# Filter taps of the next quarter computed between a convolution's forward and inverse transform, and a parameter tile that is 24 bytes longer

## The chip, the core and the metric

The kernel runs on one core of a Trainium2 chip. The metric is the device time of one execution in microseconds (us). The core's engines run side by side and meet at semaphores: TensorE (PE in the profile, with its weight loads listed as PEld), VectorE (DVE), ScalarE (ACT), GpSimd (POOL) and SyncE (SP, here only an issuer of transfers). Matrix products go from the on-chip memory SBUF through PE into PSUM, eight banks of 512 floats for each partition. DVE and ACT read PSUM and write SBUF.

## The reference

One encoder layer over 512 tokens of width 2048 in float32. The input is normalised, projected, and goes through two branches: a Hyena branch with long filters and grouped attention. The branches are gated and merged, projected again, and a feed-forward part follows. The part that the change touches is the long convolution over 1024 channels and the filter that it needs:

```python
def implicit_filter(L, w1, b1, w2, b2, w3, b3, w4, freq):
    ...
    h = jnp.sin(fr * (h @ w3.astype(f32) + b3.astype(f32)))
    h = h @ w4.astype(f32)
    ...
    decay = jnp.exp(-t[:, None] * deltas[None, :])
    h_fwd = h[:, :HYENA_W] * decay
    h_bwd = h[:, HYENA_W:] * decay
    k = jnp.concatenate([h_fwd, jnp.zeros((1, HYENA_W), f32), h_bwd[:0:-1]], axis=0)
    return k / jnp.sum(jnp.abs(k), axis=0, keepdims=True)

def bidir_fft_conv(u, k):
    L = u.shape[1]
    uf = jnp.fft.rfft(u.astype(jnp.float32), n=2 * L, axis=1)
    kf = jnp.fft.rfft(k, n=2 * L, axis=0)
    return jnp.fft.irfft(uf * kf[None], n=2 * L, axis=1)[:, :L]

def hybrid_layer(x, ...):
    h = rms_norm(x, mix_norm_g)
    proj = h @ w_in
    ...
    x0, x1, hv = jnp.split(u_h, HYENA_ORDER + 1, axis=-1)
    z = hv * x1
    z = (bidir_fft_conv(z, filt) + hy_bias * z)
    y_h = z * x0
    ...                                   # attention y_a, gates g_h, g_a
    merged = g_h * (y_h @ w_br_hyena) + g_a * (y_a @ w_br_attn)
    x = x + merged @ w_out
    h2 = rms_norm(x, ffn_norm_g)
    return x + (jax.nn.silu(h2 @ w_ffn_gate) * (h2 @ w_ffn_up)) @ w_ffn_down
```

## The kernel before

**Products.** Activations stand in SBUF with channels on the 128 partitions and the 512 tokens along them. Every float32 operand is split into a high part of fewer bits and the rest, each of type fp32r: ACT writes the high part (`wh`, `..h`, line 176 for weights, line 197 for activations), DVE the rest (`wl`, `..l`, lines 177 and 198). A product is then three matmuls, high by high, high by low and low by high (`mm3`). All matmuls are issued by `mm`, line 125, and all transposes on PE at line 128, in the order in which the program is written. Weights come in raw tiles `wr` of eight 128x128 blocks, in the order of use. Such a tile feeds 24 matmuls. A row `x2` in the listings below is two matmuls in a row with the same names.

**Stages.** The main stream on PE has these stages, one behind another, by the names of their results: `px` and `phv` (the Hyena projections, in four quarters of 256 channels), `kv` and `q` (attention, with `av`), `b` (branches), `g` (gates), `o` (output projection), `f` (feed-forward gate and up), `d` and `e` (down). In `g`, `f` and the two parts of the down projection, 2x2 blocks of a product are computed by seven products in place of eight (the function `seven`). These have eight X operands `X0` to `X7` that stay in SBUF (`fX0` and so on); for each block of weights there are eight matmuls 512 wide, one for each X, and eight 256 wide for the low part. Their names in the trace are `gx`, `gy`, `gz`, `fx` and so on.

**The side queue.** What the long convolutions need is written as generators. They stand in one queue, and `step()` is called once after each product (three matmuls) of the main stream. It runs the generator at the head to its next `yield n`, and then lets n steps pass. So a `yield 6` is 18 matmuls of the main stream between two parts of side work. Nothing else sets the order on PE.

For each quarter q two generators stand in the queue. `filter_gen(q)` computes the taps: `fp` is the last layer of the filter network (`hh`, `hl` its hidden values, `w4s` its weights), multiplied by the decay into `fd` and `bd` (line 356); ACT sums their absolute values, DVE makes the factor `rn` and the half sums `hs` and `hd` (lines 371 and 372). Then it pauses, transposes the half sums (`ktp`), transforms them (`kp`, with cosines and sines `CS`) and stores the spectrum `K` in device memory `kd`. `conv_gen(q)` transposes the signal, transforms it (`up`), multiplies it by the spectrum on DVE into `Y` (lines 449 to 454), and splits that into `Yt<q><fb><ph>h` and `..l`. After a `yield 6` the inverse transform runs in two halves of 16 matmuls each, `ab<q><ph><c>`, which read these splits; ACT and DVE scale and add the result into `abs` (lines 475 and 477).

**Where tiles lie.** SBUF pools are stacks from the left and from the right of each partition's memory, and each tile takes its bytes rounded up to 32. The first tile on the left is `prm` (parameters by channel, 175 floats a partition). Above it come the small constants, the weight tiles (`wr`, `wh`, `wl`), the temporary tiles, the activations of each stage, and later the split weights of the seven-product stages, all on the left. On the right lie, from the `g` stage on, a small `pad` tile, the raw tiles `wq`, and X operands in `xa` and `vp`; later `ea` with a part of the activations for `d`.

Of the kernel before, what the change touches and what calls it, by code (L numbers as in the profile page):

```python
# [11 lines left out]
F32 = mybir.dt.float32  # L12
# [5 lines left out]
P = 128  # L18
S = 512
# [4 lines left out]
NQ = 4  # L24
# [34 lines left out]
NPC = _n  # L59
# [47 lines left out]
def layer_kernel(tc, wpk, xT, par, flt, zemb, w4, decT, tb2, rope, qkg, out):  # L107
# [3 lines left out]
    cpool = tc.alloc_tile_pool(name="cpool", bufs=1)  # L111
# [9 lines left out]
    def ps_tile(name):  # L121
        return banks["pool"].tile([P, S], F32, tag="ps", bufs=banks["n"], name=name)

    def mm(out, lhsT, rhs, start, stop, **kw):
        tc.keep_in_program_order(nc.tensor.matmul(out, lhsT=lhsT, rhs=rhs, start=start, stop=stop, **kw))  # L125

    def transpose(out, src):
        tc.keep_in_program_order(nc.tensor.transpose(out, src, ident))
# [25 lines left out]
    def queue(gen):  # L154
        side["queue"].append(gen)

    def tmp(name):
        return tpool.tile([P, S], F32, tag="tmp", bufs=5, name=name)

# [34 lines left out]
    def split(pool, src, th, tl, bh, bl, name):  # L194
        hi = pool.tile([P, S], F32R, tag=th, bufs=bh, name=name + "h")
        lo = pool.tile([P, S], F32R, tag=tl, bufs=bl, name=name + "l")
        nc.scalar.copy(hi, src)
        nc.vector.tensor_tensor(lo, src, hi.bitcast(F32), ALU.subtract)
        return hi, lo
# [18 lines left out]
        return y  # L218


    prm = cpool.tile([P, NPC], F32, name="prm")
    nc.scalar.dma_start(prm, par)
    warm = cpool.tile([P, 1], F32, name="warm")
    nc.vector.memset(warm, 0.0)
# [2 lines left out]
    def pcol(name, i=0):  # L227
        a = PC[name] + i
        return prm[:, a:a + 1]
# [40 lines left out]
    def cw(name, shape, tag, bufs=1, dt=F32):  # L270
        return cv.tile(shape, dt, tag=tag, bufs=bufs, name=name)

    def work(name):
        return cw(name, [P, S], "wk", 6)

    fl = cw("fl", [P, 324], "fl")[:, :260]
    nc.scalar.dma_start(fl, flt)
    zem = tmp("zemb")
    nc.scalar.dma_start(zem[:33], zemb)
# [2 lines left out]
    def part(i, low, a, b):  # L282
        return CS[i][:, low * S + a:low * S + b]
# [37 lines left out]
            if l == 0:  # L321
                w4_parts(0)

    filt, kd = {}, {}
    w4t = {}

    def w4_load(q):
        w4t[q] = tmp(f"w4r{q}")
        for h in range(2):
            nc.scalar.dma_start(w4t[q][h * 64:(h + 1) * 64], w4[q])  # L330

    def w4_parts(q):

        w4r = w4t[q]
        w4h = tpool.tile([P, S], F32R, tag="tmp", bufs=5, name=f"w4h{q}")
        w4s = cw(f"w4s{q}", [P, 512], "w4s", 1, F32R)
        nc.scalar.copy(w4h[64:], w4r[64:])
        nc.scalar.copy(w4s[:64], w4r[:64])
        nc.vector.tensor_tensor(w4s[64:], w4r[64:], w4h[64:].bitcast(F32), ALU.subtract)
        w4t[q] = w4s  # L340

    def filter_gen(q):

        w4s = w4t.pop(q)
        rn, hs_l, hd_l = [], [], []
        for c in range(2):
            dec = cw(f"dec{q}{c}", [P, S], "dec", 1)
            nc.scalar.dma_start(dec, decT[2 * q + c])
            fd = work(f"fd{q}{c}")
            bd = cw(f"bd{q}{c}", [P, S + 1], "bd", 1)  # L350
            for half, dst in ((0, fd), (1, bd[:, :S])):
                fp = ps_tile(f"fp{q}{c}{half}")
                csl = slice(half * 256 + c * P, half * 256 + (c + 1) * P)
                mm(fp, w4s[:, csl], mlp["h"][0], True, False)
                mm(fp, w4s[:, csl], mlp["h"][1], False, True)
                nc.vector.tensor_tensor(dst, fp, dec, ALU.mult)
                yield 2
            nc.vector.memset(bd[:, S:S + 1], 0.0)
            n2 = cw(f"n2{q}{c}", [P, 2], "n2", 2)
            scr = tmp(f"scr{q}{c}")  # L360
            nc.scalar.activation(scr, fd, AF.Abs, accum_out=n2[:, 0:1])
            nc.scalar.activation(scr, bd[:, 1:], AF.Abs, accum_out=n2[:, 1:2])
            r = cw(f"rn{q}{c}", [P, 1], "rn", 4)
            nc.vector.tensor_tensor(r, n2[:, 0:1], n2[:, 1:2], ALU.add)
            nc.vector.tensor_scalar(r, r, 256.0, None, ALU.mult)
            nc.vector.reciprocal(r, r)
            rn.append(r)

            hs, hd = work(f"hs{q}{c}"), work(f"hd{q}{c}")
            for h, op in ((hs, ALU.add), (hd, ALU.subtract)):  # L370
                nc.vector.tensor_tensor(h[:, :256], fd[:, ::2], bd[:, 2::2], op)
                nc.vector.tensor_tensor(h[:, 256:], fd[:, 1::2], bd[:, 1:S:2], op)
            hs_l.append(hs)
            hd_l.append(hd)
        if q + 1 < NQ:
            w4_load(q + 1)
        yield 8 if q else 12
        if q + 1 < NQ:
            w4_parts(q + 1)
        taps = []  # L380
        for i, src in enumerate((hs_l, hd_l)):
            for j in range(2):
                tp = ps_tile(f"ktp{q}{i}{j}")
                for n in range(4):
                    o = n // 2 * 256 + j * P
                    transpose(tp[:, n * P:(n + 1) * P], src[n % 2][:, o:o + P])
                taps.append(split(cv, tp, "kh", "kl", 4, 4, f"k{i}{q}{j}"))
            yield 3
        yield 6


        kd[q] = dpool.tile([256, 6 * 256], F32, tag=f"kd{q}", bufs=1, name=f"kd{q}")
        for fb in range(2):
            g = []
            for i in range(2):
                kp = ps_tile(f"kp{q}{fb}{i}")
                for j in range(2):
                    a = j * 256 + fb * P
                    mm3(kp, part(i, 0, a, a + P), part(i, 1, a, a + P), *taps[2 * i + j], j == 0, j == 1)
                g.append(kp)  # L400
                yield 2
            cr, ci = tmp(f"kcr{q}{fb}"), tmp(f"kci{q}{fb}")
            nc.scalar.activation(cr, g[0], AF.Copy, scale=pcol("cosw", fb))
            nc.scalar.activation(ci, g[1], AF.Copy, scale=pcol("cosw", fb))
            k1, k2, k3 = (work(f"K{i}{q}{fb}") for i in range(3))
            nc.vector.scalar_tensor_tensor(k1, g[1], pcol("sinw", fb), cr, ALU.mult, ALU.add)
            nc.vector.scalar_tensor_tensor(k2, g[0], pcol("nsinw", fb), ci, ALU.mult, ALU.add)
            nc.vector.scalar_tensor_tensor(k3[:, :256], g[1][:, 256:], pcol("nsinw", fb), cr[:, 256:], ALU.mult, ALU.add)
            nc.vector.scalar_tensor_tensor(k3[:, 256:], g[0][:, 256:], pcol("sinw", fb), ci[:, 256:], ALU.mult, ALU.add)
            rows = kd[q][fb * P:(fb + 1) * P]  # L410
            nc.gpsimd.dma_start(rows[:, :S], k3)
            for i, k in enumerate((k1, k2)):
                nc.gpsimd.dma_start(rows[:, S:].rearrange("p (a b c) -> p a b c", a=2, b=2)[:, :, i],
                                    k.rearrange("p (a c) -> p a c", a=2))
        filt[q] = rn
# [3 lines left out]
    def conv_gen(q):  # L419

        rn = filt[q]
# [12 lines left out]
        for fb in range(2):  # L434
# [10 lines left out]
            for ph in range(2):  # L445
# [8 lines left out]
                nc.vector.tensor_tensor(y.rearrange("p (f c) -> p f c", f=2), u[:, 0], u[:, 1], ALU.add)  # L454
                ys[ph, fb] = split(r3, y, "r", "r", 16, 16, f"Yt{q}{fb}{ph}")
                yield 5
        yield 6
        abs_ = [work(f"abs{2 * q + c}") for c in range(2)]
        for ph in range(2):
            ab = [ps_tile(f"ab{q}{ph}{c}") for c in range(2)]  # L460
            for fb in range(2):
                yhi, ylo = ys[ph, fb]
                for c in range(2):
                    for i in range(2):
                        csl = slice(i * 256 + c * P, i * 256 + (c + 1) * P)
                        a = fb * 256
                        both = CS[i].rearrange("p (h t) -> p h t", h=2)[:, :, a:a + P]
                        o = ab[c][:, i * 256:(i + 1) * 256]
                        mm(o, yhi[:, csl], both, fb == 0 and i == 0, False, skip_group_check=True)
                        mm(o[:, :P], ylo[:, csl], part(i, 0, a, a + P), False, fb == 1 and i == 1, skip_group_check=True)  # L470
            yield 2
            for c in range(2):
                low = tmp(f"abl{q}{ph}{c}")[:, :256].rearrange("p (i t) -> p i t", i=2)
                src = ab[c].rearrange("p (i h t) -> p i h t", i=2, h=2)
                nc.scalar.activation(low, src[:, :, 1], AF.Copy, scale=rn[c])
                dst = abs_[c].rearrange("p (i s t) -> p i s t", i=2, s=2)[:, :, ph]
                nc.vector.scalar_tensor_tensor(dst, src[:, :, 0], rn[c], low, ALU.mult, ALU.add)
# [15 lines left out]
    xps = [ps_tile(f"px{i}") for i in range(XW)]  # L493
    xg, acc1 = [], work("acc1")
    queue(mlp_gen())
    queue(filter_gen(0))
    w00 = wblk()
    for k in range(KT):
# [887 lines left out]
```

## Time and profile before

| | us |
|---|---|
| median of 3 runs | 2547.15 |
| lowest and highest | 2546.93, 2549.27 |
| profiled execution | 2545.9 |
| its span, first to last instruction | 2544.1 |
| mean granted clock of PE | 0.998 of full |

The profile is of one execution. A row of waits names the engine, what it was about to run, the instruction that let it go, and the us in total, the number of times and the longest. A row of a window has the stretch (us from the start of the span), its length, then for each of PE, PEld, DVE, ACT and POOL the busy us and the number of instructions, then PEclk (1.00 is full speed), the busy share of the transfer engines, and GB/s. A row of a timeline has start, us, engine, line, operation, result and operands. A matmul of 512 columns shows 0.39 us from start to end, but consecutive ones overlap: the spacing of their starts is what they cost.

### The profile page before, as it was taken

The page shows a single profiled execution, that of the slowest core. Times are in us where ns is not written, and L with a number is a line of the kernel's source. Part 1 is how long each engine was busy: PE and PEld are TensorE (multiplying, and loading weights), DVE is VectorE, ACT ScalarE, POOL GpSimd, SP SyncE. Part 2 cuts the span into 40 slices and gives each one's busy share as a digit, 9 for nine tenths or more (in the row PEclk, how much of TensorE's full clock was granted, in tenths as well). Part 3 has the DMA queues.
Part 4 walks back from the last instruction along what each step waited for, and adds up shares of the span by engine and source line. Part 5 has one row for each costly group of instructions (what it writes and reads, how often), then busy time and mean ns, then how long its engine had stood idle before and what let it go on. Part 6 is the DMA issues. An engine that isn't in the chain of part 4 may idle for free.

```text
span 2544.1 us, 34631 instructions
## 1 busy us (share of the span) xinstructions
PE 2522.7 (99%) x13246; PEld 2151.3 (85%) x13246; DVE 2071.8 (81%) x2933; ACT 1180.5 (46%) x1755; POOL 176.6 (7%) x287
## 2 busy tenths in 40 slices
PE   9999999999999999999999999999999999999999
PEld 7878788888888888888888888888888888888888
DVE  7788884856569999654899899989998988987887
ACT  5433333655445454443544444444444445445443
POOL 0000001110000000000000000000000002001111
PEclk9999999999999999999999999999999999999999
DMA  6334343222544434644333333333333349647754
GB/s 211 119 107 135 123 138 114 81 89 98 185 151 159 152 137 158 203 157 149 112 104 125 116 123 126 110 131 116 125 125 116 119 148 218 165 125 188 181 153 116
DMA packets 113282, 350.42 MB, mean 138 GB/s; under 512 B 13723, under 2 KB 15003, under 8 KB 112892
## 3 DMA queue, kind: packets, MB, share of 16 engines
q1 hardware_dynamic: 70128, 248.02, 29.7%
q0 software_dynamic: 22576, 63.19, 9.3%
q10 hardware_dynamic: 20412, 37.00, 4.7%
q8 instruction: 104, 1.70, 0.3%
q14 instruction: 62, 0.51, 0.1%
HBM read 297.56 MB, written 54.26 MB: 138 GB/s over the span
## 4 chain that ended last, share of the span: by engine, by line
PE 92%; DVE 5%; issue 1%; ACT 1%; POOL 0%; DVEq 0%; ACTq 0%; POOLq 0%
PE fx L125 19%; PE fy L125 10%; PE o L125 7%; PE px L125 7%; PE b L125 6%; PE gx L125 6%; PE d L125 5%; PE fz L125 5%; PE dx L125 3%; PE ex L125 3%; PE q L125 3%; PE gy L125 3%; PE phv L125 2%; PE ey L125 2%; PE dy L125 2%; PE gz L125 2%
## 5 line engine op out<-in xcount | busy, mean ns | idle before, releaser
L177 DVE TENSOR_TENSOR wl<-wr,wh 128x1024 fp32r<-128x1024 f32 (+1 forms) x168 | 201.0, 1198 | 137.9 <-ACT wh L176 137.1
L176 ACT CAST wh<-wr 128x1024 fp32r<-128x1024 f32 (+1 forms) x168 | 173.3, 1032 | 297.2 <-PE o L125 66.4
L861 ACT CAST fwhs<-fs 128x1024 fp32r<-128x1024 f32 x176 | 184.7, 1049 | 93.5 <-PE fz L125 69.9
L863 DVE TENSOR_TENSOR fwls<-fs,fwhs 128x1024 fp32r<-128x1024 f32 x176 | 214.7, 1220 | 15.2 <-ACT fwhs L861 15.1
L861 ACT CAST fwha<-fa 128x1024 fp32r<-128x1024 f32 x132 | 138.8, 1052 | 153.9 <-PE fx L125 84.6
L125 PE MATMUL px<-xh,wh 128*128 128x512 f32 x576 | 183.3, 400 | 0.0
L125 PE MATMUL fx<-fX,fwhs 128*128 128x512 f32 x704 | 178.0, 395 | 0.6 <-DVE fv L893 0.6
L125 PE MATMUL fy<-fX,fwhs 128*128 128x512 f32 x704 | 178.2, 395 | 0.0
L125 PE MATMUL fx<-fX,fwha 128*128 128x512 f32 x704 | 174.7, 395 | 1.3 <-DVE c L990 1.3
L863 DVE TENSOR_TENSOR fwla<-fa,fwha 128x1024 fp32r<-128x1024 f32 x132 | 161.4, 1223 | 10.2 <-ACT fwha L861 9.6
L125 PE MATMUL o<-ms,wh 128*128 128x512 f32 x512 | 157.8, 389 | 0.0
L125 PEld LDWEIGHTS fx<-fX,fwha 128*128 128x128 f32 x704 | 129.1, 188 | 29.0 <-issue 1.9
L125 PEld LDWEIGHTS fx<-fX,fwhs 128*128 128x128 f32 x704 | 129.1, 188 | 28.1 <-DVE fv L893 0.9
L125 PEld LDWEIGHTS fy<-fX,fwhs 128*128 128x128 f32 x704 | 129.0, 188 | 27.4 <-DVE fv L893 0.4
L125 PEld LDWEIGHTS px<-xh,wh 128*128 128x128 f32 x576 | 108.9, 192 | 24.5 <-issue 2.4
L125 PE MATMUL d<-act,wh 128*128 128x512 f32 x384 | 120.5, 395 | 0.0
L125 PE MATMUL px<-xh,wl 128*128 128x512 f32 x288 | 114.2, 397 | 0.0
L125 PEld LDWEIGHTS o<-ms,wh 128*128 128x128 f32 x512 | 96.1, 188 | 20.0
L854 DVE TENSOR_TENSOR fs<-fa,fa 128x1024 f32<-128x1024 f32 x88 | 107.4, 1220 | 4.6 <-DMA fa<-wpk 2.4
L854 DVE TENSOR_TENSOR fs<-fs,fa 128x1024 f32<-128x1024 f32 x88 | 107.3, 1220 | 0.9 <-PE o L125 0.2
L125 PE MATMUL o<-ms,wl 128*128 128x512 f32 x256 | 99.7, 389 | 0.0
L125 PE MATMUL fx<-fX,fwls 128*128 128x256 f32 x704 | 97.4, 281 | 0.2 <-DVE fwls L863 0.2
(1088 smaller groups left out, 5917.7 us busy)
## 6 DMA issues: line engine op xcount, KB each, us to landing
fa<-wpk SPq DMA_DIRECT2D x176, 512.0 KB, 3.7
wr<-wpk SPq DMA_DIRECT2D x162, 512.0 KB, 3.5
ga<-wpk SPq DMA_DIRECT2D x60, 512.0 KB, 4.3
da<-wpk SPq DMA_DIRECT2D x32, 512.0 KB, 4.3
ea<-wpk SPq DMA_DIRECT2D x32, 512.0 KB, 4.2
actd<-c POOLq DMA_DIRECT2D x41, 256.0 KB, 4.0
actr<-actd ACTq DMA_DIRECT2D x41, 256.0 KB, 4.4
kc<-kd POOLq DMA_DIRECT2D x16, 512.0 KB, 4.1
```

The lines of the kernel that those rows point to most:

```text
L125: tc.keep_in_program_order(nc.tensor.matmul(out, lhsT=lhsT, rhs=rhs, start=start, stop=stop, **kw))
L176: nc.scalar.copy(st["hi"][:, c], st["raw"][:, c])
L177: nc.vector.tensor_tensor(st["lo"][:, c], st["raw"][:, c], st["hi"][:, c].bitcast(F32), ALU.subtract)
L854: raws["sum"] = nc.vector.tensor_tensor(t, a, b, ALU.add).ins
L861: nc.scalar.copy(hi, w)
L863: raws["wl"] = nc.vector.tensor_tensor(lo, w, hi.bitcast(F32), ALU.subtract).ins
```

## The change

Three things change.

1. `filter_gen` is cut in two. Its first part, from `fp` to the half sums, becomes `taps_gen`. For the first quarter it is queued alone, with a pause of 12 steps behind it. For the quarters after it, `conv_gen(q)` runs `taps_gen(q + 1)` between its forward and its inverse transform. The pause ahead of the inverse goes from 6 steps to 8, or 14 in the last quarter, which has no taps to compute; that between a half's matmuls and their evaluation from 2 to 4. In `filter_gen` the pause of 8 or 12 steps goes, and the split of the next quarter's `w4` moves behind the tap transposes.
2. Buffers follow what lives longer: `wk` has 7 instead of 6, `n2` 3 instead of 2, and `fl` loses 64 floats of padding.
3. `prm` has 181 floats instead of 175, of which 175 are used: 724 bytes instead of 700, a slot of 736 instead of 704.

```diff
+    def pause(n):
+        yield n
...
-    prm = cpool.tile([P, NPC], F32, name="prm")
+    prm = cpool.tile([P, NPC + 6], F32, name="prm")[:, :NPC]
...
-        return cw(name, [P, S], "wk", 6)
+        return cw(name, [P, S], "wk", 7)
 
-    fl = cw("fl", [P, 324], "fl")[:, :260]
+    fl = cw("fl", [P, 260], "fl")
...
-    def filter_gen(q):
+    def taps_gen(q):
...
-            n2 = cw(f"n2{q}{c}", [P, 2], "n2", 2)
+            n2 = cw(f"n2{q}{c}", [P, 2], "n2", 3)
...
             hs_l.append(hs)
             hd_l.append(hd)
+        folded[q] = rn, hs_l, hd_l
+
+    def filter_gen(q):
+        rn, hs_l, hd_l = folded.pop(q)
         if q + 1 < NQ:
             w4_load(q + 1)
-        yield 8 if q else 12
-        if q + 1 < NQ:
-            w4_parts(q + 1)
         taps = []
...
             yield 3
+        if q + 1 < NQ:
+            w4_parts(q + 1)
         yield 6
...
                 ys[ph, fb] = split(r3, y, "r", "r", 16, 16, f"Yt{q}{fb}{ph}")
                 yield 5
-        yield 6
+        if q + 1 < NQ:
+            yield from taps_gen(q + 1)
+        yield 8 if q + 1 < NQ else 14
         abs_ = [work(f"abs{2 * q + c}") for c in range(2)]
...
-            yield 2
+            yield 4
             for c in range(2):
...
     queue(mlp_gen())
+    queue(taps_gen(0))
+    queue(pause(12))
     queue(filter_gen(0))
```

The order of PE changes from the first taps to the `kv` product and is the same from `q` on; so are those of the other engines, and that of SP is the same throughout. On PE at the end of quarter 2's convolution, the taps of quarter 3 (`fp3..`) stand behind the inverse before:

```order
L125 MATMUL ab211_2638<-CS1_529,Yt211h_2544 128x256
L125 MATMUL ab211_2638<-CS1_529,Yt211l_2545 128x128
L125 MATMUL px17_2565<-xh11_397,wh41_2597 128x512 x2
L125 MATMUL px17_2565<-xh11_397,wl41_2598 128x512
L125 MATMUL px17_2565<-xh12_417,wh41_2597 128x512 x2
L125 MATMUL px17_2565<-xh12_417,wl41_2598 128x512
...
L125 MATMUL px17_2565<-xh14_481,wl41_2598 128x512
L125 MATMUL fp300_2687<-hh_627,w4s3_2191 128x512
L125 MATMUL fp300_2687<-hl_628,w4s3_2191 128x512
```

After, they stand ahead of it, here among the first products of `px17`, when no `ab` of this quarter has run:

```order
L125 MATMUL phv6_2445<-xh15_507,wl39_2514 128x512
L125 MATMUL px17_2565<-xh0_121,wh40_2567 128x512 x2
L125 MATMUL px17_2565<-xh0_121,wl40_2568 128x512
L125 MATMUL fp300_2579<-hh_627,w4s3_2239 128x512
L125 MATMUL fp300_2579<-hl_628,w4s3_2239 128x512
L125 MATMUL px17_2565<-xh1_142,wh40_2567 128x512 x2
L125 MATMUL px17_2565<-xh1_142,wl40_2568 128x512
L125 MATMUL px17_2565<-xh2_168,wh40_2567 128x512 x2
L125 MATMUL px17_2565<-xh2_168,wl40_2568 128x512
L125 MATMUL fp301_2589<-hh_627,w4s3_2239 128x512
```

Between the last `up` and the first `ab` stand 48 matmuls before, and 86 after (78 of the main stream and 8 `fp`) in quarters 0 to 2; in quarter 3 it is 48 and 72. On DVE around the last spectrum of quarter 2, before, where steps of the inverse (`abs`) stand about the last split `Yt211l`:

```order
L454 TENSOR_TENSOR Y211_2542<-cu211_2536 128x512
L564 TENSOR_TENSOR zf6_2562<-z6_2560 128x256 x2
L477 SCALAR_TENSOR_TENSOR abs4_2605<-ab200_2607,rn20_2095,abl200_2631 128x2x128
L198 TENSOR_TENSOR Yt211l_2545<-Y211_2542,Yt211h_2544 128x512
L477 SCALAR_TENSOR_TENSOR abs5_2606<-ab201_2608,rn21_2140,abl201_2634 128x2x128
L177 TENSOR_TENSOR wl42_2703<-wr42_2701,wh42_2702 128x1024
```

And after, where the products of the taps stand there instead, and `abs` comes later (line numbers are those of the changed kernel):

```order
L460 TENSOR_TENSOR Y211_2536<-cu211_2530 128x512
L574 TENSOR_TENSOR zf6_2562<-z6_2560 128x256 x2
L359 TENSOR_TENSOR fd30_2577<-fp300_2579,dec30_2575 128x512
L201 TENSOR_TENSOR Yt211l_2539<-Y211_2536,Yt211h_2538 128x512
L359 TENSOR_TENSOR bd30_2578<-fp301_2589,dec30_2575 128x512
L180 TENSOR_TENSOR wl41_2637<-wr41_2635,wh41_2636 128x1024
```

One product of the taps is now ahead of the last split, in the place of one step of the inverse.

More of the change, by code (lines that the diff above doesn't have):

```diff
@@ L322, in mlp_gen @@
                 w4_parts(0)
-    filt, kd = {}, {}
+    filt, kd, folded = {}, {}, {}
     w4t = {}
```

## The prediction

> **What bounds the kernel now.** I read the page first: engine shares, then the chain of work that ended last.
>
> ```profile
> span 2544.1 us, 34631 instructions
> ...
> PE 2522.7 (99%) x13246; PEld 2151.3 (85%) x13246; DVE 2071.8 (81%) x2933; ACT 1180.5 (46%) x1755; POOL 176.6 (7%) x287
> ...
> PE 92%; DVE 5%; issue 1%; ACT 1%; POOL 0%; DVEq 0%; ACTq 0%; POOLq 0%
> ```
>
> TensorE (PE) is the bound: 2522.7 of 2544.1 us busy, 92% of the chain. So time can come from two sources only: the 21 us in which PE is not busy, and the spacing of its matmuls while it is. The change touches both. The waits of PE in the stretch of the four convolutions (140 to 380 us), rows of the longest and of some short ones:
>
> ```profile
> PE ab L125 <- ACT Yt011h L197: 2.5, 1, 2.5
> PE ab L125 <- ACT Yt111h L197: 1.9, 1, 1.9
> PE ab L125 <- ACT Yt211h L197: 1.5, 1, 1.5
> PE ab L125 <- ACT Yt311h L197: 0.7, 1, 0.7
> PE ab L125 <- DVE Yt010l L198: 0.7, 1, 0.7
> ```
>
> Every one is an `ab` matmul (inverse transform) that waits for a split of a product spectrum, `Yt<quarter>..`; the first digit is the quarter. All eleven rows of that view sum to 9.5 us. What the stretches lose in all is seen in windows: length, busy us and count of each engine, granted clock (PEclk), DMA share, GB/s.
>
> ```profile
> 147.56:157.40 9.84, 5.97 (x40) 5.03 (x38) 9.78 (x15) 4.14 (x7) 0.00 (x0) 1.00 0.41 147
> 220.26:233.73 13.47, 11.28 (x51) 9.55 (x50) 13.47 (x23) 4.20 (x7) 0.00 (x0) 0.75 0.35 118
> 293.84:306.60 12.76, 10.26 (x51) 8.64 (x50) 12.09 (x23) 3.42 (x7) 0.00 (x0) 0.87 0.12 41
> 366.69:373.26 6.57, 5.53 (x39) 4.91 (x38) 5.63 (x9) 1.81 (x4) 0.00 (x0) 1.00 0.31 107
> 366.69:368.50 1.81, 1.81 (x17) 1.81 (x16) 1.81 (x3) 0.26 (x1) 0.00 (x0) 1.00 0.24 97
> 1060.00:1220.00 160.00, 160.00 (x708) 132.51 (x707) 82.77 (x102) 65.58 (x87) 8.11 (x15) 1.00 0.47 155
> ```
>
> The columns of busy time are PE, its weight loads, DVE, ACT, POOL. The fifth row is one `ab` half without a wait: 16 matmuls, 1.81 us. The last is the `o` products, 512 wide and nothing else: 160 us over 706 matmuls (708 less the two that only reach in) is 226.6 ns each. The first and the fourth stretch hold two `ab` halves and 6 matmuls of the main stream between them: 2 x 1.81 + 6 x 0.2266 = 4.98 us if nothing waited. The second and third hold 12 matmuls more, 7.70. Lost: 4.86 + 5.77 + 5.06 + 1.59 = 17.3 us. Part of it is a slow clock behind the wait, here in quarter 1 and at its end (start, us, instruction):
>
> ```profile
> 228.72 1.16 PE L125 MATMUL px<-xh,wh 128*128 128x512 f32 x2
> ...
> 230.10 1.05 PE L125 MATMUL px<-xh,wh 128*128 128x512 f32 x2
> ...
> 233.73 0.40 PE L125 MATMUL fp<-hh,w4s 128*128 128x512 f32 x1
> ```
>
> The 12 `px` matmuls from 228.72 to 233.73 took 5.01 us instead of 12 x 0.2266 = 2.72, so 2.3 us went to the clock. In the second row of the windows PEclk is 0.75.
>
> The Trainium skill ("TensorE: Matmul & The Clock Gate", Part 1: The HAM clock gate) says that the clock halves after at least one idle window of about 3.4 us. The waits above are at most 2.5 us and the clock fell all the same, so this trace does not fit a count of full idle time; taken at its word the dip would have another cause and could stay, and the forecast would be some 3 us higher.
>
> **The change, part by part.**
>
> *Taps between forward and inverse.* Nothing is added or removed: the same 8 `fp` matmuls, products, sums and loads of each quarter run earlier. In PE's order, 48 matmuls stand between the last `up` and the first `ab` now; after, 78 of the main stream and the 8 `fp`, so 86, in quarters 0 to 2. PE comes to the inverse 38 x 0.2266 = 8.6 us later; quarter 3 has 72 for 48, 5.4 us. The pause between the halves grows from 6 to 12 matmuls, another 1.4 us for the second half. What DVE must do first also grows:
>
> ```profile
> 154.43 0.68 DVE L454 TENSOR_TENSOR Y<-cu 128x512 f32<-128x512 f32 x1
> 155.03 0.86 DVE L477 SCALAR_TENSOR_TENSOR abs<-ab,rn,abl 128x256 f32<-128x256 f32 x2
> 155.82 0.67 DVE L198 TENSOR_TENSOR Yt011l<-Y,Yt011h 128x512 fp32r<-128x512 f32 x1
> ...
> L356 DVE TENSOR_TENSOR fd<-fp,dec 128x512 f32<-128x512 f32 x2 | 1.4, 688 | 0.0
> L371 DVE TENSOR_TENSOR hs<-fd,bd 128x256 f32<-128x256 f32 x3 | 1.3, 419 | 0.0
> L364 DVE TENSOR_TENSOR rn<-n 128x1 f32<-128x1 f32 x3 | 0.5, 155 | 0.2 <-ACT scr L362 0.2
> L177 DVE TENSOR_TENSOR wl<-wr,wh 128x1024 fp32r<-128x1024 f32 x11 | 13.4, 1222 | 1.5 <-ACT wh L176 1.5
> ```
>
> (Three rows of DVE's timeline in quarter 0, four of its groups from 165 to 240 us: count, busy us and mean ns of one.) A quarter's taps are 4 products of 0.688, 8 half sums of 0.419 and 6 small ones of 0.155: 7.0 us on DVE. In the new order only a product, 0.69, stands between `Y211` and `Yt211l`, where an `abs` step of 0.43 stood (0.86 for two in the row). The main stream's 38 matmuls also need 1.6 more weight splits `wl`, 1.2 us each. So DVE brings the last split 0.3 + 1.9 = 2.2 us later, PE asks 8.6 later: 6.4 us of relief against losses of at most 5.8. If all 7.0 us of the taps went ahead of it, relief would be 8.6 + 1.4 - 7.0 - 1.9 = 1.1 us, and most of the waits would stay. DVE's `abs` and the rest then lie behind the inverse; DVE was busy as follows between inverses and does the same work in less time:
>
> ```profile
> 160.00:215.00 55.00, 55.00 (x254) 45.40 (x253) 45.59 (x77) 21.99 (x34) 6.15 (x10) 1.00 0.46 149
> 235.00:290.00 55.00, 55.00 (x255) 45.33 (x254) 41.47 (x67) 21.74 (x33) 6.15 (x10) 1.00 0.44 149
> 306.00:360.00 54.00, 54.00 (x250) 44.55 (x249) 44.01 (x71) 20.29 (x32) 6.18 (x10) 1.00 0.47 151
> ```
>
> It has 10 to 13 us free in each, where the 7.0 us fit. Of the 17.3 us I take back 15.5; the ends are 17.3 and about 3 (all taps ahead). SP's order is unchanged. The decay loads on ACT's queue and the `w4` load come earlier by the same 20 us, ahead of work that does not wait for them. `wk` 7 instead of 6 and `n2` 3 instead of 2 only hold what lives longer: nothing on the path. At the start, `pause(12)` stands where `yield 12` stood: nothing, since PE has the main stream there. The `ab` of quarter 3 comes 30 matmuls later, and 108 of `kv` still follow: no flush.
>
> *The parameter tile.* 175 floats are 700 bytes, a slot of 704; 181 are 724, a slot of 736. So every tile that is stacked from the left moves up by 32 bytes, and those from the right (the raw weights `wq` and X operands of the right side, `vp`, `ea`) stay. Before, left tiles begin on a multiple of 64 bytes, right ones 32 off it; after, both are 32 off. The lone streams `px`, `kv`, `q`, `b`, `o` had both operands on the left, and stay alike. The seven-product stages (`g`, `f`, `d`, `e`) draw five of their eight X operands from the right and weights from the left; `d` takes half its activations from the right. The rows:
>
> ```profile
> 1300.00:1900.00 600.00, 600.00 (x3428) 523.77 (x3427) 542.48 (x707) 274.34 (x367) 16.75 (x31) 1.00 0.37 122
> 1588.60:1590.49 1.89, 1.89 (x18) 1.88 (x17) 1.86 (x3) 1.32 (x2) 0.00 (x0) 1.00 0.00 0
> 2095.00:2155.00 60.00, 60.00 (x260) 48.56 (x259) 48.36 (x66) 33.16 (x49) 12.63 (x15) 1.00 0.93 232
> ...
> 510.03 0.28 PE L125 MATMUL av<-pt040sl,vh 128*128 128x256 f32 x1
> ...
> 511.23 0.28 PE L125 MATMUL av<-pt041sh,vl 128*128 128x256 f32 x1
> ```
>
> In the first row half the matmuls are 512 and half 256 wide: 600 / 1713 pairs = 350.2 ns. The second is 16 of the 256-wide: 118.1 each. That leaves 232.1 for a 512-wide one. The third (`d`, 512 wide): 60 / 258 = 232.6. So the spacing is 6 ns above that of `o` wherever the two operands start differently. If alike starts give `o`'s spacing, a pair costs 226.6, plus 120 as in `av`, whose operands are alike (511.23 less 510.03, ten of them), plus the turns between widths. A turn I price from the six `kp` matmuls, whose weights are 32 off, below: 1.40 us for six is 0.04 over 6 x 0.2266 for two turns; a turn in 16 pairs is then 1.3 ns, and I take 1.7. New pair 348.3, gain 1.9 ns.
>
> ```profile
> 110.28 0.39 PE L125 MATMUL kp<-k000h,CS 128*128 128x512 f32 x1
> ...
> 111.68 0.62 PE L125 MATMUL px<-xh,wh 128*128 128x512 f32 x2
> ...
> 751.31:1048.33 297.02, 295.87 (x1681) 256.51 (x1680) 272.20 (x362) 149.49 (x201) 8.11 (x15) 1.00 0.45 154
> 1222.44:2090.79 868.35, 866.14 (x4946) 755.03 (x4945) 786.00 (x1033) 404.10 (x542) 22.16 (x41) 1.00 0.37 120
> 2157.65:2315.22 157.57, 157.43 (x897) 137.10 (x896) 141.09 (x187) 70.46 (x94) 12.90 (x15) 1.00 0.54 145
> 2382.09:2539.42 157.33, 157.33 (x897) 136.99 (x895) 138.07 (x185) 65.69 (x86) 20.55 (x29) 1.00 0.54 141
> ```
>
> The four stages hold 8421 matmuls, 4210 pairs: 1.9 ns x 4210 = 8 us. Ends: none (0), and 5.5 ns a pair (the 256-wide stay at 118.1, no turns), 23 us. `d` has 576 matmuls: 6 ns x 576 = 3.5 us. Together I take 11.5.
>
> **Sum.** 2545.9 (profiled execution: 2544.1 of span, 1.8 around it) - 15.5 - 8 - 3.5 = 2518.9. That execution is 1.25 us below the median of 2547.15, so 2520 as a median.
>
> **Rivals.**
>
> *The layout is neutral.* The 6 ns come from elsewhere (the mixture of widths, operands from many tiles), and only the waits go: 2545.9 - 15.5 + 1.25 = 2531.7. For it: I see a correlation with starts, not a test of them. Against: `d` is 512 wide throughout, as `o` is, and costs 6 ns more. The Trainium skill ("TensorE: Matmul & The Clock Gate", Part 2, Step-by-step: what each phase is for) gives PE two independent SBUF read ports, so that a weight load takes nothing from the streaming operand; by that a difference of starts between the two could not cost, and the result would be this rival's. No row before tells them apart.
>
> *Starts 32 off cost by themselves (slower).* Then `px`, `q`, `b`, `o` lose 6 ns too, and so do the three of eight X operands that were on 64: three eighths of the 4210 pairs, 1580, and some 3,700 lone 512-wide matmuls (of the 13246 - 8421 outside the pairs) x 6 ns = 32 us, less 15.5: about 2564. It decides from 15.5 / 5280 = 2.9 ns a matmul. For it: each slow stretch has an operand 32 off. Against: the `fp` matmul has both operands 32 off and took no more; its two, from 90.31 to 90.77, are 0.46 us, 0.23 each:
>
> ```profile
> 90.31 0.39 PE L125 MATMUL fp<-hh,w4s 128*128 128x512 f32 x1
> ...
> 90.77 0.63 PE L125 MATMUL phv<-xh,wh 128*128 128x512 f32 x2
> ```
>
> *The waits move.* DVE was solid before each inverse (13.47 of 13.47 in quarter 1's row); with taps there as well, `wl` or the splits come late elsewhere. Relief of 1.1 us instead of 6.4 takes back about 4 of 17.3, and without a gain by layout the time is 2543.
>
> **How the numbers follow.** Both gains 0.55, own range 2508 to 2532; layout neutral 0.23; slower by starts 0.11; waits move 0.11. 0.2% is 5 us, about what can be told from no change. Faster holds the first two and half of the last, 0.83; same 0.06; slower 0.11. The range 2506 to 2552 leaves out the slower case and the far ends of the first.
>
> **What would show it.** `ab` gone from PE's waits and PEclk 1.00 at every inverse: the first step right. `d` at 226.6 and the pair at 348 or less: the second; both unchanged: neutral. `o` above 226.6: the slower rival. Waits of PE for `wl` or `abs` between 140 and 380 us: the fourth. I am wrong if the pair grows or the waits stay at several us a quarter.

## The result and the profile after

The changed kernel takes 2531.72 us (median of 4 runs, 2529.8 to 2534.81) against 2547.04 before: a ratio of 0.9939, 95% interval 0.9922 to 0.9957. The forecast was 2520, within 2506 to 2552. The profiled execution took 2530.6, 15.3 us less than that of before. First the page:

```profile
span 2528.8 us, 34628 instructions
...
PE 2506.5 (99%) x13246; PEld 2154.7 (85%) x13246; DVE 2069.5 (82%) x2933; ACT 1180.6 (47%) x1755; POOL 176.7 (7%) x287
```

And all of PE's waits from 140 to 400 us:

```profile
PE px L125 <- DVE wl L180: 9.5, 3, 5.7
```

The eleven waits of `ab` have gone, all of them. In their place stands one row: `px`, the main stream, waits for a weight split `wl` three times, 9.5 us in all. That is as much as the `ab` rows had summed to. All the same PE came further in that time. Windows from 140 to 400 us, of before and then of the changed kernel:

```profile
140.00:400.00 260.00, 250.40 (x1165) 207.49 (x1165) 209.87 (x334) 91.71 (x138) 21.87 (x38) 0.98 0.38 126
140.00:400.00 260.00, 250.51 (x1188) 208.13 (x1187) 214.01 (x346) 95.87 (x160) 22.37 (x39) 0.99 0.39 128
```

PE is idle for 9.6 us in the first and 9.5 in the second, yet the second holds 23 matmuls more, 5.2 us at 226.6 ns each. A part of it is the granted clock. PE worked for 6.52 + 3.41 = 9.9 us at half clock before and for 3.08 in the changed kernel (rows in the section after next). Half of the difference, 3.4 us, is an estimate of what that gave; where the rest comes from is not shown. Over the whole run, busy time of PE also fell, by 16.2 us with the same 13246 matmuls. Windows of the seven-product stage `f`, of `d` and of `o`, as shown of before:

```profile
1300.00:1900.00 600.00, 600.00 (x3452) 530.31 (x3452) 545.77 (x711) 277.44 (x371) 16.78 (x31) 1.00 0.37 123
2083.00:2136.00 53.00, 53.00 (x236) 43.88 (x235) 43.78 (x60) 31.39 (x47) 11.76 (x14) 1.00 0.93 242
1060.00:1210.00 150.00, 150.00 (x664) 124.20 (x663) 75.96 (x96) 60.38 (x82) 8.12 (x15) 1.00 0.48 156
```

A pair in `f` costs 600 / 1725 = 347.8 ns (350.2 before), a `d` matmul 53 / 234 = 226.5 (232.6), and an `o` matmul 150 / 662 = 226.6, as it did. So the layout gained in the stages whose operands came partly from the left and partly from the right, and cost nothing in `o`, where both are on the left.

How much each part gave can be read at a point behind all that was reordered, the first `av` matmul that reads `pt040sh`, before and after (one row of each timeline; the first is of before):

```profile
509.92 0.28 PE L125 MATMUL av<-pt040sh,vh 128*128 128x256 f32 x1
```

```profile
504.74 0.28 PE L125 MATMUL av<-pt040sh,vh 128*128 128x256 f32 x1
```

Up to there the new order saved 5.2 us. From there to the end of the span it is 2544.1 - 509.92 = 2034.2 us before and 2528.8 - 504.74 = 2024.1 after: 10.1 us, from the layout, as the order there is the same.

Where the new waits come from is seen in the longest one. PE, DVE and ACT in quarter 2 (three timelines of the changed kernel, in this order; in square brackets the idle time ahead and who ended it):

```profile
288.93 0.61 PE L125 MATMUL px<-xh,wh 128*128 128x512 f32 x2
295.23 0.80 PE L125 MATMUL px<-xh,wl 128*128 128x512 f32 x1 [5.68 <-DVE wl L180]
295.82 1.05 PE L125 MATMUL px<-xh,wh 128*128 128x512 f32 x2
...
292.16 0.68 DVE L359 TENSOR_TENSOR fd<-fp,dec 128x512 f32<-128x512 f32 x1
292.76 0.68 DVE L201 TENSOR_TENSOR Yt211l<-Y,Yt211h 128x512 fp32r<-128x512 f32 x1
293.36 0.68 DVE L359 TENSOR_TENSOR bd<-fp,dec 128x512 f32<-128x512 f32 x1
293.96 1.21 DVE L180 TENSOR_TENSOR wl<-wr,wh 128x1024 fp32r<-128x1024 f32 x1
...
276.14 1.05 ACT L179 CAST wh<-wr 128x1024 fp32r<-128x1024 f32 x1 [3.02 <-issue]
```

The split is `wl41`. In ACT's order `wh41` is the cast at 276.14, between the first two `Yt` casts of the quarter, so all that `wl41` needs was there at 277.2. DVE ran it at 293.96, 16.8 us later: it stands in DVE's list behind the whole product spectrum and the first products of the taps. Behind the wait PE also runs at half clock for a while (1.05 us for two `px` matmuls, 0.61 ahead of it).

### The profile page after: what moved, and what is told of

It reads as the page before. It is cut to its first block, busy times and chain, and to the rows that moved or that the text cites. A ratio compares the mean times of both kernels' runs of the same rounds, so it can differ in the third digit from the quotient of the medians.

```text
span 2528.8 us, 34628 instructions
## 1 busy us (share of the span) xinstructions
PE 2506.5 (99%) x13246; PEld 2154.7 (85%) x13246; DVE 2069.5 (82%) x2933; ACT 1180.6 (47%) x1755; POOL 176.7 (7%) x287
## 4 chain that ended last, share of the span: by engine, by line
PE 93%; DVE 4%; issue 1%; DMA 1%; ACT 1%; POOL 0%; ACTq 0%; DVEq 0%; POOLq 0%; SPq 0%
PE fx L125 19%; PE fy L125 10%; PE px L125 7%; PE o L125 7%; PE b L125 6%; PE gx L125 6%; PE d L125 5%; PE fz L125 5%; PE dx L125 3%; PE ex L125 3%; PE q L125 3%; PE gy L125 3%; PE ey L125 2%; PE kv L125 2%; PE dy L125 2%; PE gz L125 2%
```

## The experiments

Each kernel was timed in turn with the kernel before on the same chip. Its ratio is to before.

**1. The longer tile alone.**

```diff
-    prm = cpool.tile([P, NPC], F32, name="prm")
+    prm = cpool.tile([P, NPC + 6], F32, name="prm")[:, :NPC]
```

> The kernel before with only the parameter tile lengthened by 24 bytes, so that in the seven-product stages and in d both operands of every matmul start 32 bytes off a multiple of 64. Theory (unlike starts of the two operands cost, alike ones do not): d falls from 232 to 227 ns, a pair of the seven-product stages from 350 to 348, in all 10 to 11 us, so about 2536.5 us; the waits of ab stay. Rival (the layout is neutral and the whole gain is from the order): 2547.

Measured 2536.94 us against 2547.76, ratio 0.9962 (0.9950 to 0.9975). PE's waits are those of before, the longest again:

```profile
PE ab L125 <- ACT Yt011h L197: 2.5, 1, 2.5
```

So some two thirds of the change's gain come from 24 bytes in a tile.

**2. The new order alone:** the changed kernel with `prm` at `NPC` floats.

> The changed kernel with the parameter tile at its old length: the new order alone. Theory: the waits of ab are gone, 9.5 us of waits of px for weight splits stand in their place, d and the pair keep 232 and 350 ns; about 2547 less 5, so 2542. Rival (layout neutral): 2531.7.

Measured 2541.98, ratio 0.9979 (0.9970 to 0.9988), as expected; of PE's waits from 140 to 400 us `px` for `wl` is the only row, 10.1 us in three waits. Together the two parts give 10.8 + 5.8 = 16.6 us, the change 15.3: the parts add up within the runs' scatter.

**3. The other side moved.** The kernel before, with the tiles on the right shifted in place of those on the left.

```diff
-    pad_t = pad.tile([P, 112], F32, name="pad_t")
+    pad_t = pad.tile([P, 120], F32, name="pad_t")
```

> The kernel before with the pad tile on the right 32 bytes longer (120 floats for 112): the right tiles move instead of the left ones, and in the seven-product stages and d both operands start on a multiple of 64. Theory (only the difference between the two operands counts): the same gain as from moving the left, 10 to 11 us, 2536.5, d 227 ns. Rival (a start 32 off is what is good): no gain, 2547. Rival (a start 32 off costs by itself): more gain here than from moving the left, below 2536.

Measured 2538.75, ratio 0.9966 (0.9953 to 0.9978): the same gain as in 1 within the intervals, with the operands of these stages on a multiple of 64 bytes in place of 32 off.

**4. Both sides moved,** so that the starts differ again, the other way round.

```diff
-    prm = cpool.tile([P, NPC], F32, name="prm")
+    prm = cpool.tile([P, NPC + 6], F32, name="prm")[:, :NPC]
...
-    pad_t = pad.tile([P, 112], F32, name="pad_t")
+    pad_t = pad.tile([P, 104], F32, name="pad_t")
```

> The kernel before with the longer parameter tile, and the pad tile on the right 32 bytes shorter (104 floats for 112): left and right tiles both move, so that the starts are unlike again, now with the left ones 32 off and the right ones on 64. First theory (only unlike starts cost): no gain, 2547 us, d at 232 ns. Second theory (left tiles 32 off are good by themselves): 2537, d at 227 ns.

Measured 2547.98, ratio 1.0000 (0.9992 to 1.0009): the gain is gone. Windows of 50 us within `d` (PE busy and count, PEclk, DMA share, GB/s) and of `f` (the columns as above), first of experiment 1:

```profile
2092.00:2142.00 50.00, 50.00 (x222) 1.00 0.93 238
...
1300.00:1900.00 600.00, 599.99 (x3444) 529.56 (x3443) 544.46 (x711) 276.17 (x369) 16.75 (x31) 1.00 0.38 123
```

Of experiment 3, the right side moved:

```profile
2092.00:2142.00 50.00, 50.00 (x222) 1.00 0.94 239
...
1300.00:1900.00 600.00, 600.00 (x3452) 530.54 (x3451) 545.85 (x710) 276.85 (x371) 16.76 (x31) 1.00 0.37 122
```

Of experiment 4, both moved:

```profile
2100.00:2150.00 50.00, 50.00 (x217) 1.00 0.92 237
...
1300.00:1900.00 600.00, 599.35 (x3424) 522.65 (x3423) 541.36 (x705) 274.41 (x367) 16.76 (x31) 1.00 0.37 121
```

And of experiment 2, the order alone:

```profile
2096.00:2146.00 50.00, 50.00 (x217) 1.00 0.93 236
...
1300.00:1900.00 600.00, 600.00 (x3433) 524.27 (x3432) 543.43 (x706) 275.36 (x369) 16.76 (x31) 1.00 0.37 122
```

`d` is 50 / 220 = 227.3 ns where the tiles of both sides start alike (1 and 3, whichever start it is) and 50 / 215 = 232.6 where they don't (4 and 2, whichever side is 32 off). In `f` 3444 and 3452 matmuls fit in 600 us with like starts, 3424 and 3433 with unlike ones. What counts is how the two sides lie to each other, not the start of either side by itself.

It is not shown that only a matmul with unlike starts pays. In `d` a group takes its six activations in the order 3, 4, 5 (on the left, as the weights are) and 0, 1, 2 (on the right). Windows of the kernel before, from the first matmul of 0 to the first of 3, and from there to the next of 0 (each counts one that only reaches in):

```profile
2105.39:2107.49 2.10, 2.10 (x10) 1.69 (x9) 2.07 (x5) 1.47 (x2) 0.53 (x1) 1.00 0.86 213
2107.49:2109.57 2.08, 2.08 (x10) 1.69 (x9) 2.08 (x2) 1.66 (x1) 0.00 (x0) 1.00 1.07 282
```

The nine matmuls with unlike starts took 2.10 us, 233 ns each. The nine behind them, whose starts are alike, took 2.08, 231 each, where nine at 226.6 would take 2.04. So in a stage that mixes both, the alike ones lose most of it too. It may be unlike starts that cost, with an effect on the matmuls behind, or the change from one start to another along the moving operands: each of these layouts has both or neither, and no run here tells them apart.

A further layout was to show whether any shift of the stack moves the time: `prm` 56 bytes longer, so that all left tiles move by 64 bytes and keep their start, expected at 2547 us. It did not fit into SBUF (`vp` needs 21 kb a partition, 20.97 were left) and so was not measured. In all layouts here the two sides are as far apart as before (2 and 4) or 32 bytes nearer (1 and 3); that multiples of 64 are what matters is not tested.

**5. Pauses alone.** The kernel of experiment 1 with the inverse put off as far as in the change, while the taps stay behind it. The pause of 8 steps between the taps and their transposes was dropped too, to make room.

```diff
-        yield 8 if q else 12
+        yield 1 if q else 12
...
-        yield 6
+        yield 19 if q + 1 < NQ else 14
         abs_ = [work(f"abs{2 * q + c}") for c in range(2)]
...
-            yield 2
+            yield 4
             for c in range(2):
```

> The kernel before with the longer parameter tile and pauses alone: the inverse is put off by as many matmuls as in the changed kernel (87 after the last up), the taps stay behind it. First theory (the taps, computed ahead of the inverse, push the weight splits back on DVE): ab waits for nothing, px for nothing, 2520 to 2523 us. Second theory (DVE is full in these stretches whatever stands there, or the scheduler's list puts splits late in any case): several us of waits for weight splits, about 2530. Where nothing but the layout counts: 2537.

Measured 2550.88, ratio 1.0017 (1.0008 to 1.0026), 14 us worse than the layout alone; neither theory had it. PE's waits from 140 to 400 us:

```profile
PE ktp L128 <- DVE hs L371: 6.8, 3, 2.7
PE px L125 <- DVE wl L177: 5.7, 3, 4.6
PE ktp L128 <- DVE rn L365: 1.4, 1, 1.4
```

`ab` waits for nothing here either. But the tap transposes `ktp` now come right behind the taps and wait for the half sums, 8.2 us. The rest stands where the convolutions end late, at 420 us, when the attention begins (PE's waits in the same trace, from 0 to 760 us):

```profile
PE kT0p L128 <- issue: 4.4, 1, 4.4
```

Of this run the missing pause is my edit's own doing, and it says little of what a plain delay would cost. But in the changed kernel, with the taps ahead of the inverse, `ktp` has no pause of its own either and waits for nothing: its half sums are there in time. Splits `wl` are late here too, with no taps ahead of them: 5.7 us. So it does not take the taps to make them late; the longer pauses do it too.

**6. The weight splits earlier in DVE's list.** The changed kernel, PE's order untouched:

```diff
-            nc.vector.tensor_tensor(st["lo"][:, c], st["raw"][:, c], st["hi"][:, c].bitcast(F32), ALU.subtract)
+            with tc.high_priority(offset=60) if 20 <= i + 1 <= 60 else nullcontext():
+                nc.vector.tensor_tensor(st["lo"][:, c], st["raw"][:, c], st["hi"][:, c].bitcast(F32), ALU.subtract)
```

> The changed kernel with the low-part weight splits wl of the quarters given a higher priority when DVE's order is made; PE's order is the same. First theory (the split for px stood behind the product spectrum and the taps in DVE's list, 10 us after its raw weights were there): the 9.5 us of waits of px and the half clock behind them go, about 2521 us. Second theory (DVE has no time to spare there): the waits come back as waits of ab for the spectra, or at the next split, 2528 to 2533.

Measured 2520.36 us, ratio 0.9897 (0.9884 to 0.9911). It is the fastest here, 11 us below the changed kernel. All that is left of PE's waits from 140 to 400 us:

```profile
PE phv L125 <- DVE wl L181: 1.7, 1, 1.7
```

DVE's timeline at the split `wl41` and at the last split of the product spectrum:

```profile
278.62 1.22 DVE L181 TENSOR_TENSOR wl<-wr,wh 128x1024 fp32r<-128x1024 f32 x1
...
289.35 0.69 DVE L202 TENSOR_TENSOR Yt211l<-Y,Yt211h 128x512 fp32r<-128x512 f32 x1
```

`wl41` runs at 278.62, and the spectrum that it was moved ahead of still arrives in time: no `ab` waits. (What stood in my expectation, that the split came 10 us after its weights, was too little; it was 16.8 us after its cast.) DVE had the room; only its order was wrong.

**7. The taps moved, with the old pauses:** the changed kernel with `yield 6` ahead of the inverse in every quarter, and `yield 2` between its halves.

> The changed kernel with the old pauses (6 steps ahead of the inverse in every quarter, 2 between the halves), the taps moved as in the change. First theory (the taps' own 24 matmuls of main stream and 8 of their own are the relief, the pauses add little): no ab waits over 1 us, waits for weight splits as in the changed kernel, 2530 to 2534 us. Second theory (the longer pauses are needed): ab waits of 1 to 2 us a quarter, 2536 or more.

Measured 2534.67, ratio 0.9956 (0.9943 to 0.9970). Waits of PE, the longest and those of `ab`:

```profile
PE phv L125 <- DVE wl L180: 4.9, 1, 4.9
...
PE ab L125 <- ACT Yt311h L200: 1.6, 1, 1.6
PE ab L125 <- DVE Yt311l L201: 0.3, 1, 0.3
```

In quarters 0 to 2 `ab` waits for nothing: the taps alone are relief enough, and the longer pause there is not needed for `ab`. In quarter 3, which has no taps to compute, 1.9 us are lost: there the pause of 14 is what does it. The splits are late here as well. The time, between those of the two theories, cannot be told from the changed kernel's; it is the waits that decide.

**8. The same priority without the move of the taps:** experiment 1 with the priority of experiment 6.

> The kernel before with the longer parameter tile and the same priority for the weight splits, without the move of the taps. First theory (the splits were in time there, and PE waits for the spectra; the move of the taps is what takes those waits away): as with the longer tile alone, 2537 us, ab waits of 9.5 us as before. Second theory (the place of the weight splits alone decides): 2525 or less.

Measured 2535.36, ratio 0.9953 (0.9941 to 0.9966), within the scatter of experiment 1's 2536.94. The waits of `ab` are there, the first and the fourth of them:

```profile
PE ab L125 <- ACT Yt111h L198: 1.9, 1, 1.9
...
PE ab L125 <- DVE Yt211l L199: 1.4, 1, 1.4
```

So the move of the taps does take away the waits for the spectra, and the priority is worth something only behind it.

**9. A still higher priority:** experiment 6 with an offset of 150.

> The changed kernel with a still higher priority of the weight splits (offset 150 where 60 made 2520): they stand ahead of their raw weights' landing, so that DVE waits for them in its order. First theory (a split has a best place: after its weights have landed, before PE needs it): DVE waits longer for wh, the spectra come later, and part of the gain is lost, 2521 to 2527 us. Second theory (the earlier the better, DVE has room): 2520 or less.

Measured 2520.74, ratio 0.9891 (0.9876 to 0.9906): the same as experiment 6. The first theory failed. DVE's waits for `wh` between 140 and 400 us, of experiment 6 and then of this one:

```profile
DVE wl L181 <- ACT wh L179: 16.1, 9, 6.5
```

```profile
DVE wl L181 <- ACT wh L179: 14.7, 9, 5.9
```

Placing the splits still earlier did not make DVE wait more, and gained nothing either.

## Why the prediction was right, and where not

The range held the time, and the direction was right. The likeliest case, both gains in full, was 2520; the time came out at 2531.7, which is to 0.1 us the rival "the layout is neutral". That rival is nevertheless false. The agreement is an accident: 10 us of gain by layout that the rival denies stand against 10 us of waits that it did not know. Only the rows of `d` and of the pairs tell the two apart, and experiments 1 to 4 settle it.

- *The layout* (8 us in the pairs, 3.5 in `d`, 11.5 in all): measured 10.1 after the cut at `av`, 10.8 as a run by itself. The pair fell to 347.8 where 348.3 was reckoned, `d` to 226.5 for 226.6. The whole stage `f`, from its first matmul to the first of `d`, went from 868.35 us to 863.18. `o`, the row for the slower rival, did not move. The size was right, but two readings under it were not. The sum charged 6 ns to all 576 matmuls of `d`, though by the prediction's own account only half of its activations lie on the right; by "wherever the two operands start differently" it would have been half of 3.5. It came out because the other half is slow there as well (231 ns, experiment 4), which the prediction did not know: that is luck. And the price of a turn was taken from six `kp` matmuls, whose starts are unlike by the same account; six times 6 ns is already the whole 0.04 us. A pair at 347.8 leaves 1.2 ns for the turns, where 1.7 were taken.
- *The waits of `ab`* (15.5 of 17.3 to come back): all of them went, as the matmuls between `up` and `ab` were counted to do. But 5.2 us net came of it.
- *The failed step* is the one on DVE: "It has 10 to 13 us free in each, where the 7.0 us fit". (By its rows it is 9.4 to 13.5.) That is an average over 55 us, while PE waits on one place in a list. The scheduler had put `wl41` behind the spectrum and the taps. The sum counted the 1.6 more splits as something that delays the last `Yt`, and never asked when a split itself would be there. It could have been seen: the order of DVE shown with the change has `wl41` behind `Yt211l` after, and `wl42` at that place before. One tile number less at that place means that this split comes one tile later in DVE's list.
- *The rival of moving waits* named "`wl` or the splits come late elsewhere", which is what happened. But its price of 2543 left out the gain by layout, so no case held the combination that came true. With the gain by layout in it, the rival would have stood at 2543 - 11.5 = 2531.5, though it let most waits of `ab` stay, and none stayed.
- *The sentence on the clock gate* was to be tested by the dips going away with the waits. In experiment 6, without long waits, there is no dip: the mean granted clock is 1.000 where it was 0.998. But the dips did not follow the length of a wait alone. Before, quarter 0's wait of 2.5 us had none behind it, quarter 1's of 1.9 and 0.3 had one; in experiment 1 the same wait of quarter 0 has one (PEclk 0.90 from 147.56 to 157.40 us, where it was 1.00). The stretches at half clock, two of before and then the one of the changed kernel, with PEclk 1.00 on either side of each:

```profile
226.64:233.47 6.83, 6.52 (x19) 5.30 (x19) 6.83 (x14) 2.37 (x4) 0.00 (x0) 0.50 0.40 141
301.74:305.15 3.41, 3.41 (x12) 2.93 (x12) 3.19 (x7) 0.95 (x2) 0.00 (x0) 0.50 0.32 96
291.49:298.31 6.82, 3.08 (x7) 2.49 (x8) 6.82 (x16) 2.06 (x5) 0.00 (x0) 0.50 0.36 114
```

They last 3.41 us or twice that. The Trainium skill ("TensorE: Matmul & The Clock Gate", Part 1: The HAM clock gate) says that the window which it watches runs freely, so that the point at which the clock changes depends on where in it the work falls. The trace agrees in so far as the same wait had a dip in one kernel and none in another. What the window counts, no run here shows.

The same page of the Trainium skill (Part 2, Step-by-step: what each phase is for) gives the stationary and the streaming operand read ports of their own. Experiments 1 to 4 show that the place of the one against the other nevertheless bears on the time, by about 6 ns a matmul in `d`.

What stays open: why the layout costs, and which matmuls start the loss. The runs show that it goes by how the two sides lie to each other, not through what.

## What to carry to other kernels

Where a spacing of matmuls differs between stages that are otherwise alike, compare where their operands begin, and try a shift of 32 bytes; 24 bytes in a tile at the bottom of the stack were worth 10 us here. When a step is moved ahead of a wait, look in the in-order list of the helping engine for everything that PE reads soon, not only for what it waited for before: an average of free time says nothing of a place in a list. And when a result equals a rival to the decimal, check the rows that the rival speaks of before believing it.

## What the runs showed of the hardware that was not expected

With fp32r operands and 128 rows, a 512-wide matmul costs 226.6 ns in `o`, where all operands begin alike (all on a multiple of 64 bytes before, all 32 off in the changed kernel). In `d`, where half of the moving operands begin 32 bytes off the rest, the mean is 232.6, and those that begin like the weights are slow as well. The 256-wide ones go the other way: 16 of them took 1.89 us, 118.1 each, in the kernel before, and 1.91, 119.4 each, in the changed one:

```profile
1401.83:1403.74 1.91, 1.91 (x17) 1.91 (x16) 1.91 (x2) 1.55 (x3) 0.00 (x0) 1.00 0.59 242
```
